# Moving the shift of three layer norms into the splits, and a group's sums to GpSimd, in a two-layer decoder step

## The chip, the cores and the metric

The kernel runs on one core of a Trainium2 chip. A core has five engines with a queue each: TensorE (PE in the profile, its weight loads PEld), VectorE (DVE), ScalarE (ACT), GpSimd (POOL) and SyncE (SP), which here issues most of the transfers. An engine works its queue strictly in order; what an instruction waits for, everything behind it waits for too. The metric is the device time of one execution in microseconds, lower is better. The median of the runs of the kernel before is 1148.62 us.

## The reference, cut to what matters

One step of a decoder of two layers on 512 prompt tokens and 8 sampled tokens, model width 1024: window attention, a convolutional FFN, gated linear attention (GLA), a second FFN. Behind each of the four stands a layer norm of a weighted residual:

```python
def layer_norm(x, g, b):
    xf = x.astype(jnp.float32)
    mu = jnp.mean(xf, -1, keepdims=True)
    var = jnp.mean(jnp.square(xf - mu), -1, keepdims=True)
    return ((xf - mu) * lax.rsqrt(var + LN_EPS) * g.astype(jnp.float32) + b.astype(jnp.float32)).astype(x.dtype)
...
        xp = layer_norm(ALPHA * xp + mp, ln_mix_g[i], ln_mix_b[i])
...
        fp, cp = conv_ffn(xp, buf0, ffn_w_up[i], ffn_conv_w[i], ffn_conv_b[i], ffn_w_down[i])
...
        xp = layer_norm(ALPHA * xp + fp, ln_ffn_g[i], ln_ffn_b[i])
```

All of it is computed in float32.

## The kernel before

**Tiles.** x lies transposed, 128 partitions by 8 rows of features (KD = 8) by tokens. The tokens are two groups, a with 256 and b with 256 + 8, each with its own tiles: x_a and x_b, and the split operands, xs_a (both parts in one tile) and xh_b, xl_b. For accuracy each float32 operand is split into a high part rounded to the matmul's format and a low part, the rest. A product of a weight unit (1024 by 128) is 8 times 3 matmul passes into one of four PSUM accumulators (accp): high weights by high rows (L173), high by low rows (L174), low weights by high rows (L175). Weights come by DMA into one of two raw buffers; ScalarE makes the high part wh (L158), VectorE the low part wl (L161), six units ahead of use.

**Order.** The work has six phases: attention, its output projection, FFN, GLA, its output projection, FFN. Inside a phase group a leads group b by four or five units; the products that b has left at the end of a phase stand before a's first of the next phase. One unit of one group is a slot. A step that has to come later is a generator, which yields the number of slots to wait. From this program order a scheduler with an engine model lists each engine's queue ahead of time; `issue_after` makes it put an instruction behind another one.

**A layer norm** has two parts. As each product of the projection ends, ln_chunk adds it to the row of x on VectorE (L219, L217 behind the FFN), which frees the accumulator; ScalarE squares the row (L237); the sum of the rows, s1, is built on VectorE (L247), the sum of the squares, s2, on GpSimd for rows 1 to 3, on VectorE for the others (L249). Both lie in tiles shown as s_a and s_b. The row 0 is handled first: a mean of it is subtracted from all rows (L232). When all eight rows are in, ln_end multiplies s1 and s2 by a matrix of 1/1024 (L256, outputs tp and pv), which gives the mean and the mean square on all partitions. ScalarE copies mu and squares it (L261, L262), VectorE makes the negative variance nv (L267), ScalarE Ln and Exp (L273, L274), VectorE a refinement of r = 1/sqrt (L275 to L277); the mean is subtracted from five rows on GpSimd, from three on VectorE (L263). Then for each row:

```python
            nc.vector.tensor_tensor(u, x[:, m], r, op=ALU.mult)
            nc.scalar.activation(g.xh[:, m], parted(u), AF.Identity, scale=sc(m), bias=bi(m))
            ts = nc.gpsimd.tensor_scalar(x[:, m], u, sc(m), bi(m), op0=ALU.mult, op1=ALU.add)
            nc.vector.tensor_tensor(g.xl[:, m], parted(x[:, m]), g.xh[:, m].bitcast(F32), op=ALU.subtract)
```

sc and bi are the norm's scale and shift, one value per partition. The low row needs x as GpSimd writes it.

**The next phase.** In an FFN the units alternate: a gate unit (its product copied to aext on ScalarE, L574; convolution, one step on ScalarE L579 and two on VectorE L580, L581; Gelu on ScalarE L588, with a table load where the table held another function) and a value unit (its product multiplied by the gate on VectorE, hprod L600, which frees the accumulator; split L198, L199). GLA starts with gla_rank (L671, L672), whose output leads to the decay (L685 to L699, with a scan on VectorE) and, with q (L715) and k (L722), to the attention product (L730). The last norm has its own code (`last`).

## Time and profile before

| | |
|---|---|
| median of 3 runs (lowest, highest) | 1148.62 us (1147.16, 1149.75) |
| the profiled execution | 1146.73 us |
| its span | 1144.7 us |
| mean granted TensorE clock | 0.992 of full speed |
| VectorE busy / ScalarE busy / GpSimd busy | 794.5 / 575.6 / 326.4 us |
| layer norms: first rows of the next phase's first product | at 168.0, 528.6, about 766.4 us of the span |

The profiled execution is one run, seen by the profiler; its time lies 1.89 us under the median. A row of a timeline gives start, duration, engine, line and operation, output and inputs by their names, and in brackets the idle time just before it with what ended it; a row with x2 or more joins consecutive instructions. A row of a source line gives the least, the median and the greatest duration in ns. DVE busy over a window doesn't count its queue's waits.

### The profile page before, as it was taken

The numbers are of one execution on the slowest core, as the hardware profiler recorded it, in microseconds if no ns is written. First come the engines' busy times: TensorE is split into PE (matmuls) and PEld (weight loads), VectorE is DVE, ScalarE is ACT, GpSimd is POOL, SyncE is SP. The second block draws the span as 40 slices with busy tenths as digits, with TensorE's granted clock in tenths as the row PEclk, the third lists the DMA queues.
The fourth block names the chain that finished last, engine by engine and source line by source line (L and its number), as shares of the span: only waits on it lengthen the run. The fifth ranks groups of instructions, "written<-read, shape, count | busy, mean of one in ns | idle before, by whom it ended". The sixth has DMA issues, their size and how long they took to land.

```text
span 1144.7 us, 22953 instructions
## 1 busy us (share of the span) xinstructions
PE 1104.2 (96%) x8806; PEld 1055.2 (92%) x8806; DVE 794.5 (69%) x1663; ACT 575.6 (50%) x1253; POOL 326.4 (29%) x556
## 2 busy tenths in 40 slices
PE   8999899999999999999899999989999999999995
PEld 8997798999999999998899999888999999999994
DVE  7897589655665566668867777799655665566657
ACT  5677457534553245435545556456524553245433
POOL 4575568100110011357300101287100110011344
PEclk9999999999999999999899999999999999999998
DMA  7553031323323233243124355341333232232222
GB/s 241 149 183 90 13 111 56 111 93 123 99 93 111 92 99 105 74 133 110 38 89 147 117 177 162 133 145 62 105 96 127 93 106 98 92 111 93 74 63 75
DMA packets 53789, 122.82 MB, mean 107 GB/s; under 512 B 6792, under 2 KB 27312, under 8 KB 53680
## 3 DMA queue, kind: packets, MB, share of 16 engines
q1 hardware_dynamic: 51664, 119.61, 32.4%
q10 hardware_dynamic: 2016, 1.75, 0.5%
q8 instruction: 69, 1.13, 0.4%
q14 instruction: 40, 0.33, 0.1%
HBM read 108.67 MB, written 8.47 MB: 102 GB/s over the span
## 4 chain that ended last, share of the span: by engine, by line
PE 70%; DVE 12%; DMA 6%; ACT 4%; POOL 4%; issue 4%; SPq 0%; ACTq 0%; DVEq 0%; POOLq 0%
PE accp L191 15%; PE accp L174 14%; PE accp L173 14%; PE accp L175 14%; PE accp L192 8%; DMA vb<-dv 3%; DVE wl L161 2%; POOL x_b L298 1%; DVE sgla L845 1%; DMA qs<-hl 1%; ACT wh L158 1%; POOL x_a L298 1%; DVE u L296 1%; PE pv L494 1%; DVE msq L276 1%
## 5 line engine op out<-in xcount | busy, mean ns | idle before, releaser
L161 DVE TENSOR_TENSOR wl<-raw,wh 128x1024 fp32r<-128x1024 f32 (+2 forms) x189 | 231.4, 1226 | 106.7 <-ACT wh L158 105.2
L158 ACT ACTIVATE wh<-raw 128x1024 fp32r<-128x1024 f32 (+2 forms) x185 | 191.9, 1037 | 215.0 <-PE accp L174 196.8
L173 PE MATMUL accp<-xh_b,wh 128*128 128x264 f32 x976 | 271.7, 279 | 2.5 <-DVE hprod L600 2.5
L174 PE MATMUL accp<-xl_b,wh 128*128 128x264 f32 x976 | 271.3, 278 | 0.2
L175 PE MATMUL accp<-xh_b,wl 128*128 128x264 f32 x976 | 270.8, 278 | 0.0
L191 PE MATMUL accp<-xs_a,wh 128*128 128x512 f32 x576 | 196.3, 382 | 0.0
L173 PEld LDWEIGHTS accp<-xh_b,wh 128*128 128x128 f32 x976 | 185.0, 190 | 3.5 <-DVE hprod L600 2.9
L174 PEld LDWEIGHTS accp<-xl_b,wh 128*128 128x128 f32 x976 | 184.9, 189 | 3.1 <-DVE xl_b L301 0.6
L175 PEld LDWEIGHTS accp<-xh_b,wl 128*128 128x128 f32 x976 | 184.8, 189 | 0.8 <-issue 0.6
L192 PE MATMUL accp<-xs_a,wl 128*128 128x256 f32 x576 | 145.4, 273 | 0.0
L173 PE MATMUL accp<-hh_b,wh 128*128 128x264 f32 x480 | 133.7, 279 | 3.3 <-ACT hh_b L198 3.3
L174 PE MATMUL accp<-hl_b,wh 128*128 128x264 f32 x480 | 134.3, 280 | 0.0
L175 PE MATMUL accp<-hh_b,wl 128*128 128x264 f32 x480 | 133.3, 278 | 0.0
L191 PEld LDWEIGHTS accp<-xs_a,wh 128*128 128x128 f32 x576 | 109.1, 189 | 11.4
L173 PE MATMUL accp<-xs_a,wh 128*128 128x256 f32 x400 | 112.3, 287 | 5.6 <-DVE x_b L219 2.1
L174 PE MATMUL accp<-xs_a,wh 128*128 128x256 f32 x400 | 112.4, 283 | 3.2 <-DVE xs_a L301 2.9
L192 PEld LDWEIGHTS accp<-xs_a,wl 128*128 128x128 f32 x576 | 110.2, 191 | 1.9
L175 PE MATMUL accp<-xs_a,wl 128*128 128x256 f32 x400 | 111.0, 280 | 0.7 <-DVE wl L161 0.5
L173 PEld LDWEIGHTS accp<-hh_b,wh 128*128 128x128 f32 x480 | 91.3, 190 | 3.8 <-ACT hh_b L198 3.6
L174 PEld LDWEIGHTS accp<-hl_b,wh 128*128 128x128 f32 x480 | 91.3, 190 | 1.4 <-issue 0.3
L175 PEld LDWEIGHTS accp<-hh_b,wl 128*128 128x128 f32 x480 | 91.3, 190 | 0.2
L202 POOL COPY hist<-aext 128x2 f32<-128x2 f32 x44 | 8.9, 203 | 284.4 <-DVE aext L578 281.3
(320 smaller groups left out, 2495.3 us busy)
## 6 DMA issues: line engine op xcount, KB each, us to landing
raw<-in_w_up SPq DMA_DIRECT2D x88, 512.0 KB, 3.4
raw<-in_w_down SPq DMA_DIRECT2D x32, 512.0 KB, 3.4
raw<-in_w_gla SPq DMA_DIRECT2D x24, 512.0 KB, 3.4
raw<-in_w_mix_o SPq DMA_DIRECT2D x16, 512.0 KB, 4.1
raw<-in_w_down SPq DMA_DIRECT2D x16, 384.0 KB, 3.1
qs<-hl SPq DMA_DIRECT2D x64, 64.0 KB, 2.1
sgla<-in_state_gla SPq DMA_DIRECT2D x16, 256.0 KB, 2.8
vb<-dv SPq DMA_DIRECT2D x16, 256.0 KB, 3.7
```

The lines of the kernel that those rows point to most:

```text
L158: nc.scalar.activation(h[:, c], r[:, c], AF.Copy)
L161: nc.vector.tensor_tensor(l[:, c], r[:, c], h[:, c].bitcast(F32), op=ALU.subtract)
L173: nc.tensor.matmul(o, h[:, ks], xh, start=k == 0, stop=False)
L174: nc.tensor.matmul(o, h[:, ks], xl, start=False, stop=False)
L175: nc.tensor.matmul(o, l[:, ks], xh, start=False, stop=k == nt - 1)
L191: both = lambda: nc.tensor.matmul(o, h[:, ks], in_turn(rs[:, k].rearrange("p t q j -> p t (q j)")), start=k == 0, stop=last)
L192: low = lambda: nc.tensor.matmul(o[:, :P], l[:, ks], in_turn(rh[:, k]), start=False, stop=False)
L276: nc.vector.scalar_tensor_tensor(q, q, 0.5, nv, op0=ALU.mult, op1=ALU.mult)
L296: nc.vector.tensor_tensor(u, x[:, m], r, op=ALU.mult)
L298: ts = nc.gpsimd.tensor_scalar(x[:, m], u, sc(m), bi(m), op0=ALU.mult, op1=ALU.add)
L494: mm = nc.tensor.matmul(pv[64 * v:64 * v + 64, b * P:(b + 1) * P], self.vtok[:, kb, 64 * v:64 * v + 64], parts[v][w][:, b], start=i == 0, ...
L845: late(nc.vector.scalar_tensor_tensor(s[:, j], vb[:, j], kraw[:, b:b + 1], s[:, j], op0=ALU.mult, op1=ALU.add))
```

## The change

For the first three norms (all but the last):

- The scaled row v = (x − mu)·sc·r is written into x itself. The high row is v + shift rounded; the low row is (v + shift) − high, made by one VectorE instruction from v. So neither needs GpSimd. The final addition x += shift stays on GpSimd, and its program place is 14 slots later (LATEB).
- Group b's sums s1 and s2 for rows 1 to 6 are on GpSimd; for row 7 on VectorE. Its two mean products come in the slot of the last row, not one later. Group a's are as before.
- For 5 units before the ends of three phases, the weights' low part comes one slot later in program order, and, as b's sums do, behind the last scaled row of group a where that row is at most 3 slots old (HOLD, `behind`).
- In group a's first FFN unit all passes with low rows come last in its product; in gla_rank for both groups too.
- The gelus of an FFN's first three gates are put behind Exp of the last norm in ScalarE's queue.
- The subtractions of the mean on GpSimd lose the hint that put them behind the group's last final pass.

```diff
@@ -52,6 +52,10 @@
+LATEB = 14
+
+HOLD = 3
@@ load_unit
-    def load_unit(self, u, pieces=1, extra=False):
+    def load_unit(self, u, pieces=1, extra=False, late=False):
...
-            nc.vector.tensor_tensor(l[:, c], r[:, c], h[:, c].bitcast(F32), op=ALU.subtract)
+            if not late:
+                nc.vector.tensor_tensor(l[:, c], r[:, c], h[:, c].bitcast(F32), op=ALU.subtract)
         self.w[u] = (h, l)
+        if late:
+            self.spawn(self.low_part(l[:, c], r[:, c], h[:, c]), 1)
+
+    def low_part(self, l, r, h):
+        with self.behind():
+            self.nc.vector.tensor_tensor(l, r, h.bitcast(F32), op=ALU.subtract)
+        yield from ()
@@ product
+        tail = g.i == 0 and u in self.phases[2::3]
...
             nc.tensor.matmul(o, h[:, ks], xh, start=k == 0, stop=False)
-            nc.tensor.matmul(o, h[:, ks], xl, start=False, stop=False)
-            nc.tensor.matmul(o, l[:, ks], xh, start=False, stop=k == nt - 1)
+            if not tail:
+                nc.tensor.matmul(o, h[:, ks], xl, start=False, stop=False)
+            nc.tensor.matmul(o, l[:, ks], xh, start=False, stop=not tail and k == nt - 1)
+        for k in range(nt) if tail else ():
+            nc.tensor.matmul(o, h[:, k * P:(k + 1) * P], in_turn(rl[:, k]), start=False, stop=k == nt - 1)
@@ ln_chunk
+    def behind(self):
+
+        return self.tc.issue_after(self.norm[0]) if self.norm and self.slot < self.norm[1] else ExitStack()
...
-        nc.vector.tensor_tensor(g.s1, x[:, 0] if m == 1 else g.s1, x[:, m], op=ALU.add)
-        eng = nc.gpsimd if m < S2P else nc.vector
-        eng.tensor_tensor(g.s2, g.s2, q, op=ALU.add)
+
+        p1, p2 = (KD - 1, KD - 1) if g.i and not last else (0, S2P)
+        with self.behind():
+            (nc.gpsimd if m < p1 else nc.vector).tensor_tensor(g.s1, x[:, 0] if m == 1 else g.s1, x[:, m], op=ALU.add)
+            (nc.gpsimd if m < p2 else nc.vector).tensor_tensor(g.s2, g.s2, q, op=ALU.add)
@@ ln_end
-        yield 1
+        yield 0 if g.i and not last else 1
...
-        with self.tc.issue_after(self.pool_mark) if self.pool_mark else ExitStack():
-            for m in range(2, KD) if last else range(NSUB):
-                sub(nc.gpsimd, m)
+        for m in range(2, KD) if last else range(NSUB):
+            sub(nc.gpsimd, m)
...
-        nc.scalar.activation(r, r, AF.Exp, scale=-0.5)
+        self.exp = nc.scalar.activation(r, r, AF.Exp, scale=-0.5).ins
...
-            u = t("u", 2)
-            nc.vector.tensor_tensor(u, x[:, m], r, op=ALU.mult)
-            nc.scalar.activation(g.xh[:, m], parted(u), AF.Identity, scale=sc(m), bias=bi(m))
-            ts = nc.gpsimd.tensor_scalar(x[:, m], u, sc(m), bi(m), op0=ALU.mult, op1=ALU.add)
-            if m == KD - 1:
-                self.pool_mark = ts.ins
-            nc.vector.tensor_tensor(g.xl[:, m], parted(x[:, m]), g.xh[:, m].bitcast(F32), op=ALU.subtract)
+            v = nc.vector.scalar_tensor_tensor(x[:, m], x[:, m], sc(m), r, op0=ALU.mult, op1=ALU.mult)
+            if m == KD - 1 and g.i == 0:
+                self.norm = v.ins, self.slot + HOLD
+            nc.scalar.activation(g.xh[:, m], parted(x[:, m]), AF.Identity, bias=bi(m))
+            nc.vector.scalar_tensor_tensor(g.xl[:, m], parted(x[:, m]), bi(m), g.xh[:, m].bitcast(F32), op0=ALU.add, op1=ALU.subtract)
+        yield LATEB
+        for m in range(KD):
+            nc.gpsimd.tensor_scalar(x[:, m], x[:, m], 1.0, bi(m), op0=ALU.mult, op1=ALU.add)
@@ ffn_gate
-        nc.scalar.activation(c[:, :n], c[:, :n], AF.Gelu)
+
+        with self.tc.issue_after(self.exp) if j < 3 else ExitStack():
+            nc.scalar.activation(c[:, :n], c[:, :n], AF.Gelu)
@@ gla_rank
-        for k in range(KD):
-            nc.tensor.matmul(o, w[:, k], in_turn(g.xh[:, k]), start=k == 0, stop=False)
-            nc.tensor.matmul(o, w[:, k], in_turn(g.xl[:, k]), start=False, stop=k == KD - 1)
+        for x in (g.xh, g.xl):
+            for k in range(KD):
+                nc.tensor.matmul(o, w[:, k], in_turn(x[:, k]), start=x is g.xh and k == 0, stop=x is g.xl and k == KD - 1)
@@ next_unit
-            self.load_unit(u, extra=extra)
+            done = u - WSLOTS
+            late = not extra and self.units[u][1] and any(e - 5 <= done < e for e in (*self.phases[2:3], *self.phases[3:4], *self.phases[5:6]))
+            self.load_unit(u, extra=extra, late=late)
```

In the queues, GpSimd behind the first norm, before (x_b and s_b are b's rows and sums; L249 adds squares, L263 subtracts the mean, L298 writes the final rows, L202 copies FFN history):

```order
L232 TENSOR_TENSOR x_b<-x_b,sa 128x264 x7
L249 TENSOR_TENSOR s_b<-s_b,sq 128x264 x3
L263 TENSOR_TENSOR x_a<-x_a,mu 128x256 x5
L298 TENSOR_SCALAR x_a<-u,par 128x256 x8
L263 TENSOR_TENSOR x_b<-x_b,mu 128x264 x5
L202 COPY hist<-aext 128x2
```

And now, at the same place, from b's fourth square sum on (L271 adds rows, L272 squares, L325 adds the shift, L286 subtracts the mean, L219 and L595 serve the FFN's history):

```order
L272 TENSOR_TENSOR s_b<-s_b,sq 128x264
L271 TENSOR_TENSOR s_b<-s_b,x_b 128x264
L325 TENSOR_SCALAR x_a<-x_a,par 128x256
L272 TENSOR_TENSOR s_b<-s_b,sq 128x264
L325 TENSOR_SCALAR x_a<-x_a,par 128x256 x6
L271 TENSOR_TENSOR s_b<-s_b,x_b 128x264
L325 TENSOR_SCALAR x_a<-x_a,par 128x256
L272 TENSOR_TENSOR s_b<-s_b,sq 128x264
L219 COPY hist<-aext 128x2
L595 MEMSET aext 128x2
L219 COPY hist<-aext 128x2
L286 TENSOR_TENSOR x_b<-x_b,mu 128x264 x5
```

What moved: the final passes of a, in one block between subtractions before, now lie among b's sums, six of them between its fifth and sixth row; b's mean is subtracted behind them as before.

VectorE ahead of b's nv behind the first norm, before (s_b sums, L301 low rows of a, L296 scaled rows of a, L161 weight splits, L267 nv):

```order
L247 TENSOR_TENSOR s_b<-s_b,x_b 128x264
L249 TENSOR_TENSOR s_b<-s_b,sq 128x264
L301 TENSOR_TENSOR xs_a<-x_a,xs_a 128x2x128
L296 TENSOR_TENSOR u<-x_a,r 128x256
L301 TENSOR_TENSOR xs_a<-x_a,xs_a 128x2x128
L296 TENSOR_TENSOR u<-x_a,r 128x256
L161 TENSOR_TENSOR wl<-raw,wh 128x1024
L267 SCALAR_TENSOR_TENSOR nv<-msq,pv 128x264
L263 TENSOR_TENSOR x_b<-x_b,mu 128x264
L301 TENSOR_TENSOR xs_a<-x_a,xs_a 128x2x128 x2
L275 TENSOR_TENSOR msq<-r 128x264
```

And now (L173 and L166 weight splits, L271 and L272 the seventh row's sums, L604 and L605 convolution steps, L289 nv):

```order
L173 TENSOR_TENSOR wl<-raw,wh 128x1024 x2
L271 TENSOR_TENSOR s_b<-s_b,x_b 128x264
L272 TENSOR_TENSOR s_b<-s_b,sq 128x264
L604 SCALAR_TENSOR_TENSOR conv<-aext,par,conv 128x256
L605 SCALAR_TENSOR_TENSOR conv<-aext,par,conv 128x256
L173 TENSOR_TENSOR wl<-raw,wh 128x1024
L604 SCALAR_TENSOR_TENSOR conv<-aext,par,conv 128x256
L166 TENSOR_TENSOR wl<-raw,wh 128x1024
L605 SCALAR_TENSOR_TENSOR conv<-aext,par,conv 128x256
L289 SCALAR_TENSOR_TENSOR nv<-msq,pv 128x264
L286 TENSOR_TENSOR x_b<-x_b,mu 128x264
L297 TENSOR_TENSOR msq<-r 128x264
```

What moved: a's scaled and low rows are all done ahead of this place; between b's last sum and nv stand four convolution steps and two weight splits of the FFN.

TensorE at the first product behind the first norm, before (L173 high by high, L174 high by low, L175 low by high; two rows more where two units alternate):

```order
L175 MATMUL accp<-hh_b,wl 128x264
L173 MATMUL accp<-xs_a,wh 128x256 x2
L174 MATMUL accp<-xs_a,wh 128x256
L175 MATMUL accp<-xs_a,wl 128x256
L173 MATMUL accp<-xs_a,wh 128x256
L174 MATMUL accp<-xs_a,wh 128x256
L175 MATMUL accp<-xs_a,wl 128x256
L173 MATMUL accp<-xs_a,wh 128x256 x2
L174 MATMUL accp<-xs_a,wh 128x256
L175 MATMUL accp<-xs_a,wl 128x256
```

And now, from the seventh feature row on (L187 high by high, L190 low by high, L192 low rows of the first unit, L189 those of other units):

```order
L187 MATMUL accp<-xs_a,wh 128x256
L190 MATMUL accp<-xs_a,wl 128x256
L187 MATMUL accp<-xs_a,wh 128x256
L190 MATMUL accp<-xs_a,wl 128x256
L187 MATMUL accp<-xs_a,wh 128x256
L192 MATMUL accp<-xs_a,wh 128x256
L189 MATMUL accp<-xs_a,wh 128x256
L190 MATMUL accp<-xs_a,wl 128x256
L187 MATMUL accp<-xs_a,wh 128x256
L192 MATMUL accp<-xs_a,wh 128x256
```

What moved: the first unit's high-row passes come as 16 in a row, and its low-row passes lie one by one between passes of the next unit.

2 lines of the change are left out of this document (1 added, 1 removed).

## The prediction

> **What bounds the kernel now.** I read the page first, then the windows around the layer norms, the list of what TensorE waited for, and the timelines of the four engines in the first of these windows.
>
> ```profile
> PE 1104.2 (96%) x8806; PEld 1055.2 (92%) x8806; DVE 794.5 (69%) x1663; ACT 575.6 (50%) x1253; POOL 326.4 (29%) x556
> ```
>
> TensorE is the bound, and the change takes no pass from it. Only time in which TensorE does nothing can be won. The windows behind the first three norms, from the first pass of the next phase on, hold much of it (columns: window, its length, then busy time and count of each engine):
>
> ```profile
> 167.90:207.00 39.10, 34.99 (x295) 33.69 (x294) 34.52 (x73) 25.90 (x48) 28.98 (x34) 1.00 0.26 82
> 528.60:556.00 27.40, 21.70 (x161) 19.47 (x160) 25.36 (x59) 16.40 (x33) 21.62 (x21) 0.95 0.18 59
> 766.40:806.40 40.00, 34.89 (x293) 33.38 (x291) 36.79 (x77) 27.61 (x51) 29.82 (x34) 1.00 0.26 86
> ```
>
> TensorE idles 39.10 − 34.99 = 4.1, 5.7 and 5.1 us there: 14.9 us, the most that this change can win. VectorE (third engine) is at 34.52 of 39.10, nearly as full, and GpSimd (last) at 28.98. The waits that lie there, all windows together (us, times, longest):
>
> ```profile
> PE accp L174 <- DVE xs_a L301: 2.9, 2, 1.5
> PE accp L173 <- DVE hprod L600: 2.5, 2, 1.3
> PE accp L173 <- DVE x_b L219: 2.1, 2, 1.1
> PE accp L672 <- DVE xl_b L301: 1.5, 2, 1.0
> PE accp L672 <- DVE xs_a L301: 1.3, 1, 1.3
> PE accp L173 <- DVE x_b L217: 1.1, 1, 1.1
> PE accp L173 <- ACT xs_a L297: 0.8, 1, 0.8
> ```
>
> Group a's low row (L301) comes late, because GpSimd must first write x (L298); b's last product waits for an accumulator that x_b += product has not emptied; and b's first product waits for the accumulator that hprod holds. In the first window these stand at:
>
> ```profile
> 168.00 0.38 PE L173 MATMUL accp<-xs_a,wh 128*128 128x256 f32 x2
> 169.74 0.38 PE L174 MATMUL accp<-xs_a,wh 128*128 128x256 f32 x1 [1.36 <-DVE xs_a L301]
> 176.64 0.28 PE L173 MATMUL accp<-xs_a,wh 128*128 128x256 f32 x1
> 176.75 0.61 PE L256 MATMUL tp<-s_b,ones_a 128*128 128x264 f32 x2
> 190.26 0.38 PE L173 MATMUL accp<-xh_b,wh 128*128 128x264 f32 x1 [1.26 <-DVE hprod L600]
> ```
>
> Passes start 0.11 us apart (176.64 to 176.75). The mean product for b's sums, tp, was not late: TensorE came to it at 176.75, and b's last square sum ended at 176.43 + 0.42 = 176.85.
>
> **The change part by part.** *The first group's rows.* The shift now goes into both splits, so xl needs no GpSimd. Before, on VectorE (start, duration):
>
> ```profile
> 162.86 1.75 DVE L161 TENSOR_TENSOR wl<-raw,wh 128x1024 fp32r<-128x1024 f32 x1
> 164.87 0.42 DVE L277 SCALAR_TENSOR_TENSOR r<-msq,r 128x256 f32<-128x256 f32 x1
> 165.21 0.75 DVE L263 TENSOR_TENSOR x_a<-x_a,mu 128x256 f32<-128x256 f32 x2
> 165.88 0.42 DVE L219 SCALAR_TENSOR_TENSOR x_b<-x_b,accp 128x264 f32<-128x264 f32 x1
> 166.22 0.76 DVE L296 TENSOR_TENSOR u<-x_a,r 128x256 f32<-128x256 f32 x2
> 176.43 0.42 DVE L249 TENSOR_TENSOR s_b<-s_b,sq 128x264 f32<-128x264 f32 x1
> 179.45 0.42 DVE L267 SCALAR_TENSOR_TENSOR nv<-msq,pv 128x264 f32<-128x264 f32 x1
> ```
>
> With the weight split ahead of r gone (late now), r ends near 163.6, the two subtractions (0.75) near 164.3, and eight scaled rows at 0.34 apart (a pair takes 0.76) end at 167.0. ScalarE's high rows follow, so the 16 high passes that now come first run from 168.0 without a wait. Behind the rows come two weight splits of 1.22 (below), to 169.4, x_b to 169.8, then the low rows, the first at about 170.4. TensorE asks for it after 16 passes, 168.0 + 16 × 0.11 = 169.8. So 0.7 us of the 1.36 stays, later low rows (0.34 apart) keep up with passes that lie between others, and the accumulator wait of about 1 us goes. TensorE reaches tp, 77 passes behind its first, at 168.0 + 77 × 0.11 + 0.7 = 177.2.
>
> *The second group's sums.* They move to GpSimd, in whose queue six of a's final passes (x += shift) now stand between b's fifth and sixth rows, one more ahead of the fifth's square, another ahead of the sixth's. Nothing of TensorE needs these passes, but what stands behind them feeds tp and pv. The prices:
>
> ```profile
> L298 POOL TENSOR_SCALAR x_a<-u,par x24: 917/1178/2483, 166.7 to 779.5; 128x256 f32<-128x256 f32 x24
> L298 POOL TENSOR_SCALAR x_b<-u,par x24: 651/1110/1322, 186.3 to 794.9; 128x264 f32<-128x264 f32 x24
> L249 POOL TENSOR_TENSOR s_b<-s_b,sq x12: 742/930/1473, 151.5 to 1117.9; 128x264 f32<-128x264 f32 x12
> L161 DVE TENSOR_TENSOR wl<-raw,wh x189: 414/1225/1769, 10.3 to 1107.5; 128x1024 fp32r<-128x1024 f32 x167, 128x768 fp32r<-128x768 f32 x16, 128x256 fp32r<-128x256 f32 x4, 128x512 fp32r<-128x512 f32 x2
> ```
>
> The trace shows this final pass only in its scaled form, 0.65 to 1.18 us. I take 1.03, between the least of a's rows (0.92) and the median of b's (1.11), since two weight splits lie beside the six on VectorE. From 169.8 (x_b's fifth row): sum 0.93, pass 1.03, square sum 0.93, six passes 6.2, sum 0.75, pass 0.65, square sum 0.75 (sixth row ready long before), then VectorE's own last addition 0.42: the sums are whole at S = 181.5, where before they were at 176.85. At 0.65 a pass S is 178.8, at 1.18 it is 183.5. TensorE stands at tp for about 4 us: a new wait, in place of three old ones.
>
> [...]
>
> ```profile
> 166.75 6.39 POOL L298 TENSOR_SCALAR x_a<-u,par 128x256 f32<-128x256 f32 x4 [3.22 <-DVE u L296]
> 166.89 1.22 DVE L161 TENSOR_TENSOR wl<-raw,wh 128x1024 fp32r<-128x1024 f32 x1
> ```
>
> *Behind S.* VectorE's queue now has, between b's last sum and nv, four convolution steps and two weight splits (before: nv came 2.6 us behind the sum, 176.85 to 179.45). And the gelus, with their table load, go ahead of b's scaled rows:
>
> ```profile
> 186.44 0.87 DVE L580 SCALAR_TENSOR_TENSOR conv<-aext,par,conv 128x256 f32<-128x256 f32 x2
> 179.90 0.43 ACT L273 ACTIVATE r<-nv 128x264 f32<-128x264 f32 x1 [0.63 <-DVE nv L267]
> 180.37 0.42 ACT L274 ACTIVATE r<-r 128x264 f32<-128x264 f32 x1
> 186.21 1.24 ACT L297 ACTIVATE xh_b<-u,par 128x264 fp32r<-128x264 f32 x2 [2.17 <-DVE u L296]
> 187.47 1.28 ACT L588 ACT_TABLE_LOAD   x1
> 188.76 0.42 ACT L588 ACTIVATE conv<-conv 128x256 f32<-128x256 f32 x1
> ```
>
> Four convolution steps at 0.4 apart and two splits at 1.15 make 4.0; nv to the end of Exp 1.34 (179.45 to 180.79); table and gelu 1.70; then hprod, two steps of r with the second hprod, r (1.45), two subtractions 0.75, a low part 0.35 and the first scaled row 0.42: S + 10.0, and the high row (0.6) S + 10.6 = 192.1. That is b's first pass, the 147th of the window in both kernels; before it stood at 190.26. The new order gains the hprod wait (gelu now first) and loses it again to the row: 192.1 − 190.26 = +1.8 us, less some 0.3 of small waits behind it: **+1.5 us** in the first window.
>
> The third window is built alike, without one wait that goes there besides (0.8, high row of a): **+0.7 us**. In the second no convolution lies behind S; what ends it is the attention product of a's first head:
>
> ```profile
> 528.63 0.27 PE L671 MATMUL accp<-xs_a,wh 128*128 128x256 f32 x1
> 549.76 0.38 PE L671 MATMUL accp<-xh_b,wh 128*128 128x264 f32 x1 [1.13 <-ACT v_a L739]
> 551.73 0.89 DVE L690 TENSOR_TENSOR_SCAN dcum<-reset,dmn 128x256 f32<-128x256 f32 x1
> 555.77 1.01 PE L730 MATMUL sc<-q_a,k_a 128*128 128x128 f32 x3 [0.23 <-DVE k_a L722]
> ```
>
> S lies 181.5 − 167.9 = 13.6 behind the window's start, as in the first. From there: weight split and decay step, nv, Ln and two Exp, r, the scan (0.89), first scaled row 6.5, high row 1.0, eight high rows at 0.6 with the low ones behind, q and k: 14.4. The product comes 28.0 behind the start, and before 555.77 − 528.63 = 27.1: **+0.9 us**.
>
> The rest costs nothing: the late weight splits are wanted six units on, counts of instructions per engine stay the same but for 27 sums that leave VectorE, the queue of weight loads doesn't change, and the last norm and what follows it keep their order. The final pass of x in b's rows is read again only by the next norm. If that cover were gone, it would cost what such a pass takes, about 1 us a row.
>
> Sum: 1.5 + 0.7 + 0.9 = +3.1 us on the profiled execution's 1146.73, 1149.8; on the median of 1148.62, **1151.7 us**. 0.2% of it, 2.3 us, is about what a measurement of this kernel can tell from no change.
>
> **The rivals.** *Quick GpSimd: faster.* The final passes, no longer tied to u, run at 0.65 us (the least of x_b's rows), and S is 178.8, 2.7 earlier. Each window then gains about 2.7 against the forecast: −1.2, −2.0 and −1.8, 5.0 in all, 1143.6 us. For it: beside idle VectorE 0.65 is measured. Against: a's passes never went under 0.92, and weight splits of 1.2 lie beside them. It decides at S = 180.1 or so, where the new wait costs as much as the old ones give back; under S = 177.2 TensorE would not wait at tp at all, and most of the 14.9 us could go: 1140 or less. *Stalls only move: no change.* S comes at 179.5 to 180.6; the sum is within 2.3 us of nothing, 1146.5 to 1150.8. For it: in before, too, each wait that was shorter stood ahead of another. *GpSimd at its contended rate: clearly slower.* At 1.18 a pass S is 183.5, and the windows cost +3.6, +2.8 and +3.0: 1158 us. For it: medians of 1178 and 1110 ns in before. *The sums' move doesn't relieve VectorE*, as its two-input steps slow down beside GpSimd's, as r's first step does in before while GpSimd subtracts (0.96, not 0.42):
>
> ```profile
> 181.82 0.96 DVE L275 TENSOR_TENSOR msq<-r 128x264 f32<-128x264 f32 x1
> ```
>
> This adds to the forecast rather than turning it, under 1 us a window, 1153.
>
> **How the numbers follow.** Forecast and both slower rivals: the forecast 0.28, contended 0.12, no relief 0.08. No change 0.26. Quick GpSimd 0.26, a quarter of it without any wait at tp. What of the forecast's own spread falls within 2.3 us of before goes to "same": slower 0.46, same 0.27, faster 0.27. For 8 in 10 the range takes in the quick case down to 1143.6 and the contended one almost whole: 1143.5 to 1157. The likeliest case alone: 1149.5 to 1154.
>
> **What would show it.** In the changed kernel's trace: the row of tp with a wait of about 4 us for GpSimd's sum of b in windows one and three, and GpSimd busy with x_a's final passes just ahead of it; the low row's wait down from 1.36 to under 1; no wait for hprod; b's first pass near 192. Wrong it is if tp shows no wait (S early), or if TensorE's idle time in the three windows falls under 12 us together.

## The result, and the profile after

| | before | changed |
|---|---|---|
| median | 1148.59 us (6 runs, 1147.16 to 1150.63) | 1160.13 us (6 runs, 1158.27 to 1163.10) |
| ratio | | 1.0102 (95%: 1.0082 to 1.0121) |
| the profiled execution, its span | 1146.73, 1144.7 us | 1162.86, 1161.0 us |
| mean granted TensorE clock | 0.992 | 0.978 |

Slower was forecast, by 3.1 us; it is 11.5 us. Instructions on TensorE are the same 8806, but its busy time grew by 13 us. In the changed kernel's page:

```profile
PE 1117.1 (96%) x8806; PEld 1064.9 (92%) x8806; DVE 792.1 (68%) x1636; ACT 567.2 (49%) x1253; POOL 322.0 (28%) x583
```

More busy time for the same passes means slower passes. To see where, I numbered TensorE's matmuls in both traces and took the same numbers ahead of and behind each window (1250 and 1600, 4100 and 4400, 5990 and 6400). Before they start at 157.44 and 203.23, 526.15 and 572.79, 763.77 and 819.66; in the changed kernel at 161.26 and 211.44, 534.35 and 583.68, 774.95 and 836.01. So the three windows lose 4.39, 2.70 and 5.16 us, 12.25 together. Another 3.82 was lost ahead of the first window, and 0.3 elsewhere. Ahead of the first window TensorE's 1250 matmuls come in the same order in both kernels, and in every other build of this study; the difference there lies between −0.15 and 3.82 us. In this execution TensorE is at half clock there up to 14.5 us (before, up to 10.4 at most) and for 6.8 us from 137.4 on (before, for 3.4 us). So the profiled execution, 2.7 us above the median of its kernel, carries a loss that the change need not have made.

What TensorE waited for in the changed kernel (us, times, longest):

```profile
PE accp L187 <- ACT xh_b L321: 6.9, 2, 3.8
...
PE accp L192 <- DVE xs_a L322: 1.5, 3, 1.1
PE accp L698 <- DVE xs_a L322: 1.5, 3, 1.1
PE accp L187 <- DVE x_b L240: 1.4, 2, 1.1
...
PE pv L279 <- DVE s_b L272: 0.7, 2, 0.4
```

The wait for hprod is gone, as forecast. A wait for b's high row stands in its place, 3.15 and 3.77 us long. The wait for b's sums, forecast at 4 us, is 0.4. In the first window:

```profile
171.82 0.27 PE L187 MATMUL accp<-xs_a,wh 128*128 128x256 f32 x1
...
183.77 0.61 PE L279 MATMUL tp<-s_b,ones_a 128*128 128x264 f32 x2
...
196.03 0.59 PE L187 MATMUL accp<-xh_b,wh 128*128 128x264 f32 x1 [3.15 <-ACT xh_b L321]
```

And this is what the wait brought with it (window, length, busy time and count of TensorE, weight loads, VectorE, ScalarE, GpSimd, and then the granted clock):

```profile
194.00:196.00 2.00, 0.00 (x0) 0.00 (x0) 2.00 (x6) 1.04 (x4) 0.03 (x1) 0.85 0.00 0
196.00:198.00 2.00, 1.97 (x9) 1.97 (x10) 2.00 (x6) 2.00 (x5) 0.00 (x0) 0.50 0.00 0
198.00:200.00 2.00, 2.00 (x11) 2.00 (x11) 2.00 (x6) 1.09 (x3) 0.52 (x1) 0.50 0.00 0
200.00:202.00 2.00, 2.00 (x12) 2.00 (x11) 2.00 (x6) 0.00 (x0) 2.00 (x1) 0.50 0.00 0
202.00:204.00 2.00, 2.00 (x18) 2.00 (x18) 1.40 (x4) 1.13 (x3) 2.00 (x4) 0.94 0.02 4
```

From 195.4 on TensorE is granted half its clock, for 6.8 us, and issues 9 to 12 passes in 2 us where it issues 18 at a clock of 0.94. That is the loss that the forecast had not priced. What came ahead of such a fall in these traces is in the last section.

Why b's row came late is in the queues of the other engines. GpSimd, then VectorE, then ScalarE, then what SyncE's weight loads waited for from 165 to 190 us:

```profile
176.56 5.79 POOL L325 TENSOR_SCALAR x_a<-x_a,par 128x256 f32<-128x256 f32 x6
182.31 0.74 POOL L271 TENSOR_TENSOR s_b<-s_b,x_b 128x264 f32<-128x264 f32 x1
```

```profile
173.99 4.71 DVE L322 SCALAR_TENSOR_TENSOR xs_a<-x_a,par,xs_a 128x256 fp32r<-128x256 f32 x7
...
184.53 0.43 DVE L272 TENSOR_TENSOR s_b<-s_b,sq 128x264 f32<-128x264 f32 x1 [1.01 <-POOL s_b L272]
184.88 0.48 DVE L604 SCALAR_TENSOR_TENSOR conv<-aext,par,conv 128x256 f32<-128x256 f32 x1
185.39 0.49 DVE L605 SCALAR_TENSOR_TENSOR conv<-aext,par,conv 128x256 f32<-128x256 f32 x1
185.80 1.22 DVE L173 TENSOR_TENSOR wl<-raw,wh 128x1024 fp32r<-128x1024 f32 x1
186.93 0.48 DVE L604 SCALAR_TENSOR_TENSOR conv<-aext,par,conv 128x256 f32<-128x256 f32 x1
187.41 1.23 DVE L166 TENSOR_TENSOR wl<-raw,wh 128x1024 fp32r<-128x1024 f32 x1
188.55 0.97 DVE L605 SCALAR_TENSOR_TENSOR conv<-aext,par,conv 128x256 f32<-128x256 f32 x1
189.45 0.41 DVE L289 SCALAR_TENSOR_TENSOR nv<-msq,pv 128x264 f32<-128x264 f32 x1
```

```profile
184.40 1.06 ACT L162 ACTIVATE wh<-raw 128x1024 fp32r<-128x1024 f32 x1 [2.60 <-DMA raw<-in_w_up]
...
187.27 0.36 ACT L284 COPY mu<-tp 128x264 f32<-128x264 f32 x1
187.52 0.39 ACT L285 ACTIVATE msq<-tp 128x264 f32<-128x264 f32 x1
```

```profile
SPq L160 <- DVE wl L173: 22.6, 4, 14.3
```

Six final passes stand between two of b's sums, as forecast. They took 0.96 us on average: five took 0.64 to 0.78, the last, beside two weight splits, 2.56. GpSimd and VectorE ran what is listed here in the order of their queues: b's sum behind the six passes began as the last of them ended (182.3 us). Beside GpSimd's sums and passes a low row of a takes 0.67 us. Behind b's last sum VectorE works without a pause up to nv: four convolution steps and two weight splits, as forecast.

One thing was overlooked. A late weight split holds its raw buffer (there are two), and no load was issued from 158 to 172.66 us; one waited 14.3 us for a late split. In the kernel before, the longest time from one load to the next there is 5.9 us. A later load, which had waited for a late split too, holds up ScalarE's high part by 2.60 us (184.40), and b's mean, ready at 184.4, is copied behind it and a second high part at 187.27. That is not what nv waited for, though: the squared mean was there at 187.52 + 0.39 = 187.91, 1.5 us ahead of nv, which followed VectorE's last convolution step with no idle time.

### The profile page after: what moved, and what is told of

Its sections match the earlier page's. It is cut to its first block, busy times and chain, and to the rows that moved or that the text cites. A ratio compares the mean times of both kernels' runs of the same rounds, so it can differ in the third digit from the quotient of the medians.

```text
span 1161.0 us, 22917 instructions
## 1 busy us (share of the span) xinstructions
PE 1117.1 (96%) x8806; PEld 1064.9 (92%) x8806; DVE 792.1 (68%) x1636; ACT 567.2 (49%) x1253; POOL 322.0 (28%) x583
## 3 DMA queue, kind: packets, MB, share of 16 engines
q8 instruction: 69, 1.13, 0.4%
## 4 chain that ended last, share of the span: by engine, by line
PE 78%; DVE 10%; DMA 4%; ACT 4%; issue 2%; POOL 1%; SPq 0%; ACTq 0%; DVEq 0%; POOLq 0%
PE accp L187 16%; PE accp L189 16%; PE accp L190 16%; PE accp L208 15%; PE accp L209 8%; DMA vb<-dv 2%; DMA qs<-hl 1%; DVE x_a L318 1%; ACT wh L162 1%; DVE xs_a L322 1%; DMA raw<-in_w_up 1%; PE pv L518 1%; DVE wl L173 1%; DVE wl L166 1%; PE sc L793 1%
## 5 line engine op out<-in xcount | busy, mean ns | idle before, releaser
L166 DVE TENSOR_TENSOR wl<-raw,wh 128x1024 fp32r<-128x1024 f32 (+2 forms) x174 | 210.5, 1212 | 115.4 <-ACT wh L162 114.8
L187 PE MATMUL accp<-xh_b,wh 128*128 128x264 f32 x976 | 272.6, 279 | 6.9 <-ACT xh_b L321 6.9
L189 PE MATMUL accp<-xl_b,wh 128*128 128x264 f32 x976 | 271.4, 278 | 0.0
L190 PE MATMUL accp<-xh_b,wl 128*128 128x264 f32 x976 | 270.8, 278 | 0.0
L187 PEld LDWEIGHTS accp<-xh_b,wh 128*128 128x128 f32 x976 | 185.8, 190 | 7.8 <-ACT xh_b L321 7.3
L189 PEld LDWEIGHTS accp<-xl_b,wh 128*128 128x128 f32 x976 | 185.2, 190 | 2.5 <-issue 0.4
L190 PEld LDWEIGHTS accp<-xh_b,wl 128*128 128x128 f32 x976 | 184.9, 189 | 0.9 <-issue 0.6
L209 PE MATMUL accp<-xs_a,wl 128*128 128x256 f32 x576 | 145.4, 273 | 0.0
L187 PE MATMUL accp<-hh_b,wh 128*128 128x264 f32 x480 | 134.1, 279 | 3.4 <-ACT hh_b L215 3.4
L189 PE MATMUL accp<-hl_b,wh 128*128 128x264 f32 x480 | 134.4, 280 | 0.0
L190 PE MATMUL accp<-hh_b,wl 128*128 128x264 f32 x480 | 133.5, 278 | 0.0
L187 PE MATMUL accp<-xs_a,wh 128*128 128x256 f32 x400 | 116.7, 295 | 4.9 <-DVE x_b L240 1.4
L190 PE MATMUL accp<-xs_a,wl 128*128 128x256 f32 x400 | 114.6, 289 | 0.5 <-DVE wl L166 0.5
L189 PE MATMUL accp<-xs_a,wh 128*128 128x256 f32 x384 | 111.5, 291 | 0.3 <-DVE xs_a L216 0.2
L187 PEld LDWEIGHTS accp<-hh_b,wh 128*128 128x128 f32 x480 | 91.6, 191 | 3.8 <-ACT hh_b L215 3.7
L189 PEld LDWEIGHTS accp<-hl_b,wh 128*128 128x128 f32 x480 | 91.5, 191 | 1.4 <-issue 0.3
L190 PEld LDWEIGHTS accp<-hh_b,wl 128*128 128x128 f32 x480 | 91.4, 190 | 0.2
L219 POOL COPY hist<-aext 128x2 f32<-128x2 f32 x44 | 10.0, 228 | 281.1 <-DVE aext L602 279.1
```

The source lines that it names most:

```text
L166: nc.vector.tensor_tensor(l[:, c], r[:, c], h[:, c].bitcast(F32), op=ALU.subtract)
L187: nc.tensor.matmul(o, h[:, ks], xh, start=k == 0, stop=False)
L189: nc.tensor.matmul(o, h[:, ks], xl, start=False, stop=False)
L190: nc.tensor.matmul(o, l[:, ks], xh, start=False, stop=not tail and k == nt - 1)
L209: low = lambda: nc.tensor.matmul(o[:, :P], l[:, ks], in_turn(rh[:, k]), start=False, stop=False)
```

## The experiments

Two tables of my own reading stand for all of them. First, where group b's chain is in the first window, in us behind group a's first pass, and what the window costs against before (by the same numbered matmuls, fills not counted); "sums" is the end of the last addition, the others are starts; "half" is half of the time at half clock:

```
                   sums   tp    mean   nv    row   b's first  window  half
before             8.85  8.75   9.45  11.45 17.76   22.26      0      0
changed           13.15 11.95  15.45  17.63 23.11   24.21      4.39   3.41
e1_fill           13.25 11.96  16.25  18.42 23.89   25.00      2.73   0
e2_pass_behind    11.07 11.11  14.90  16.87 22.67   23.78      3.97   3.41
e3_sums_back      12.44 14.34  15.22  16.48 22.73   23.84      2.61   1.71
e4_shift_only     12.22 15.41  17.75  19.15 25.37   26.48      5.33   5.12
e5_late_off       12.29 13.01  13.66  15.92 21.74   22.84      0.60   1.71
e7_nv_first       13.12 12.11  15.66  16.34 25.37   26.47      4.58   3.41
e11_late_gla      12.68 12.39  13.14  16.65 22.13   23.24      1.94   1.71
e12_late_gla_pass 12.11 13.06  13.71  15.38 21.15   22.38      1.03   1.71
```

Second, the cost of all three windows and of the stretch between the second and the third (GLA and what follows):

```
                  first  second  between  third
changed            4.39    2.70    0.29    5.16
e1_fill            2.73    3.78    1.48    3.25
e2_pass_behind     3.97    2.72    0.46    4.75
e3_sums_back       2.61   -0.97    6.41    4.88
e4_shift_only      5.33    2.27    0.15    5.77
e5_late_off        0.60    4.74    3.81    1.08
e6_rows_back       4.34    2.49   -0.19    3.75
e7_nv_first        4.58    2.88    1.58    5.70
e8_all_three       2.66    5.63    3.49    3.05
e9_before_fill    -0.01   -1.76    1.26    0.56
e10_fill_all       2.91    1.59   -0.17    3.36
e11_late_gla       1.94    1.87    0.03    0.89
e12_late_gla_pass  1.03    3.33   -0.12    2.35
```

"Between" holds no layer norm. It moves by up to 6 us as the scheduler lists GLA's queues anew: in the three builds that lose most there (e3, e5, e8) TensorE's order differs from the changed kernel's at 650 to 670 of 1590 places, in the others at 32 or fewer, and its waits there come to 5.7 or 5.8 us, not 1.9. So a total mixes the edit with that, and the windows are read one by one. Each is read from one execution, and a wait of 3.15 us came with 6.8 us at half clock in one, a longer wait with 3.4 in another (last section).

**e1_fill: the wait filled.**

```diff
+        if g.i and u in self.phases[2::3]:
+            fill = self.mtile("sc")[:, :g.n]
+            with self.tc.issue_after(self.lastmm):
+                for _ in range(FILL):
+                    nc.tensor.matmul(fill, self.ones_a, g.mu, start=True, stop=True)
...
```

> The changed kernel with six float32 products of ones by the mean of group b (into a free PSUM tile, result unused) put on TensorE just ahead of group b's first FFN pass behind the first and third norm, where TensorE waits 3.3 us. No other work is changed. Theory clock: the granted clock falls to 0.50 because of that wait and the 5 us behind it run at half speed; with the wait filled the clock stays at 1.00, b's first pass stands where it stood, and each of the two windows is 2 to 2.9 us shorter, 1155 us in all. Rival rows: the slow stretch is only TensorE waiting for the high and low rows of b, whatever the clock; then the fill changes nothing, 1160 us.

Measured: 1157.57 us, ratio to before 1.0077 (1.0055 to 1.0099), 2.6 less than the changed kernel. The row behind the fill, and the clock there:

```profile
192.84 0.38 PE L193 MATMUL accp<-xh_b,wh 128*128 128x264 f32 x1 [1.17 <-ACT xh_b L328]
```

```profile
194.00:196.00 2.00, 2.00 (x18) 1.82 (x17) 2.00 (x6) 1.78 (x5) 0.00 (x0) 1.00 0.00 0
196.00:198.00 2.00, 1.74 (x16) 1.73 (x16) 2.00 (x6) 0.38 (x1) 1.68 (x1) 1.00 0.00 0
```

The clock holds, and the first window costs exactly what b's first pass is late: 25.00 − 22.26 = 2.74, measured 2.73. In the changed kernel it is late by 1.95, and the window costs 4.39. So 2.44 of the 4.39 is the clock's. In the third window, too, the clock holds (1.00) and the cost is the lateness: b's first pass is 801.04 − 789.94 − 7.83 = 3.27 later, where 7.83 was lost ahead of the window, and the window costs 3.25. The two windows are 1.7 and 1.9 us shorter, not the 2 to 2.9 expected, as b's row itself came 0.8 later in this build. The second window and the stretch behind it lost 2.3 more, so the total fell less still: 2.6 us, with intervals that overlap.

**e2_pass_behind: a's final passes behind b's last GpSimd sum.**

```diff
+            s2i = (nc.gpsimd if m < p2 else nc.vector).tensor_tensor(g.s2, g.s2, q, op=ALU.add)
+        if g.i and m == KD - 2:
+            self.bsum = s2i.ins
...
+        with self.tc.issue_after(self.bsum):
+            for m in range(KD):
+                nc.gpsimd.tensor_scalar(x[:, m], x[:, m], 1.0, bi(m), op0=ALU.mult, op1=ALU.add)
```

> The changed kernel with group a's final passes (x += shift, GpSimd) put behind group b's last sum on GpSimd. Theory queue and port: the passes among the sums and beside the low rows cost both; without them a's seven low rows take 2.5 us rather than 4.7, the sums are whole some 4 us earlier, b's first pass waits under 1.5 us, the clock does not fall, and the time is 1146 to 1151 us. Rival tail: what comes behind the sums (convolution steps, weight splits, gelu ahead of the rows) sets the wait alone; then the wait shrinks by under 1 us and the time stays over 1157 us.

Measured: 1158.27 us, 1.0079 (1.0060 to 1.0097). The sums are whole 2.1 us earlier (11.07 for 13.15), and b's first pass comes 0.4 earlier. The rival was right: what lies behind the sums sets it. The mean stayed at 14.90, behind ScalarE's high parts, and nv behind convolution steps and splits. The expectation of 1146 to 1151 us failed: it had taken the sums for the bound.

**e3_sums_back: b's sums on the engines they had before.**

```diff
-        p1, p2 = (KD - 1, KD - 1) if g.i and not last else (0, S2P)
+        p1, p2 = 0, S2P
```

> The changed kernel with group b's sums on the engines they had before (s1 on VectorE, s2 for rows 1 to 3 on GpSimd). Theory queue and port: the final passes still run beside a's low rows, and VectorE gets nine more additions ahead of nv, so b's first pass comes no earlier: 1157 to 1162 us. Rival: GpSimd's slow sums are the loss; then the time falls to 1152 us or less.

Measured: 1161.21 us, 1.0108 (1.0086 to 1.0129): as the first theory had it in total, but not in its parts. The sums were whole 0.7 us earlier and b's first pass came 0.4 earlier. The first window cost 2.61, mostly because 3.4 us of it are at half clock where the changed kernel has 6.8. The second gained 0.97, but in another order: a's attention product came 20.89 us behind the window's start, ahead of b's first GLA pass, where before it came at 27.14. And 6.4 was lost in the stretch between. What the sums' place on GpSimd costs by itself this run doesn't show.

**e4_shift_only: the kernel before with the shift in the splits alone.**

```diff
-            u = t("u", 2)
-            nc.vector.tensor_tensor(u, x[:, m], r, op=ALU.mult)
...
+            nc.vector.scalar_tensor_tensor(x[:, m], x[:, m], sc(m), r, op0=ALU.mult, op1=ALU.mult)
+            nc.scalar.activation(g.xh[:, m], parted(x[:, m]), AF.Identity, bias=bi(m))
+            nc.vector.scalar_tensor_tensor(g.xl[:, m], parted(x[:, m]), bi(m), g.xh[:, m].bitcast(F32), op0=ALU.add, op1=ALU.subtract)
+            ts = nc.gpsimd.tensor_scalar(x[:, m], x[:, m], 1.0, bi(m), op0=ALU.mult, op1=ALU.add)
```

> The kernel before with the shift in the splits alone (scaled row in place, low row made without GpSimd, final pass on GpSimd behind it); sums, weight splits, order of passes and gelus as before. Forecast's step: the low rows' waits go in part and nothing else moves, 1145 to 1148 us. Rival port: the low rows slow down beside the final passes as in the changed kernel (0.67 us each), the waits stay, 1148 to 1151 us.

Measured: 1160.87 us, 1.0100 (1.0075 to 1.0124). Neither expectation came near. Its VectorE, TensorE and ScalarE in the first window:

```profile
166.45 2.85 DVE L295 SCALAR_TENSOR_TENSOR x_a<-x_a,par,r 128x256 f32<-128x256 f32 x7
...
171.44 0.47 DVE L297 SCALAR_TENSOR_TENSOR xs_a<-x_a,par,xs_a 128x256 fp32r<-128x256 f32 x1
```

```profile
171.97 0.58 PE L174 MATMUL accp<-xs_a,wh 128*128 128x256 f32 x1 [3.37 <-DVE xs_a L297]
```

```profile
187.91 1.28 ACT L273 ACT_TABLE_LOAD   x1
189.20 0.42 ACT L273 ACTIVATE r<-nv 128x264 f32<-128x264 f32 x1
189.64 1.28 ACT L274 ACT_TABLE_LOAD   x1
```

With GpSimd out of the low row's way, the scheduler lists all of a's scaled rows ahead of the first low row (171.44; before 169.26), and TensorE, which wants that low row for its third pass, waits 3.37 us and is granted half its clock for 6.8 us, from 171.1 on. A gelu now stands ahead of Ln and Exp, which costs two more table loads (1.28 us each) on b's chain. The other parts of the change (low passes last, the gelu hint) are aimed at just these two, and the changed kernel's total is where this one's is.

**e5_late_off: no late weight splits.**

```diff
-            late = not extra and self.units[u][1] and any(e - 5 <= done < e for e in (*self.phases[2:3], *self.phases[3:4], *self.phases[5:6]))
+            late = False and not extra and self.units[u][1] and any(e - 5 <= done < e for e in (*self.phases[2:3], *self.phases[3:4], *self.phases[5:6]))
```

> The changed kernel with no late weight splits (the low part of every unit right behind its high part in program order). Theory buffers: a late split holds its raw buffer, so the next load, the high part and with it the mean's copy behind it on ScalarE come late; without it group b's mean is copied 1 us earlier, b's first pass comes earlier, 1156 to 1159 us. Rival rows: splits ahead of group a's rows cost more than that, 1161 us or over.

Measured: 1157.95 us, 1.0072 (1.0051 to 1.0093). The mean is copied 1.8 us earlier (13.66), b's first pass comes 1.4 earlier, and the FFN windows cost 0.60 and 1.08 where they cost 4.39 and 5.16: 7.9 us won, the largest share of any part. The second window (+2.0) and the stretch behind it (+3.5) give most of it back; e11 below, with late splits there alone, loses neither. The buffers do come free sooner: the longest time from one load to the next ahead of the first window's sums falls from 14.7 to 8.3 us. But the mean is not what nv waited for here either: the squared mean was there 1.6 us ahead of it. What also changed is VectorE's queue, where one weight split stands between b's last sum and nv, not two. So these runs show what the late splits cost, and not whether it is the held buffer or the split's new place on VectorE.

**e6_rows_back: passes in the old order.**

```diff
-        tail = g.i == 0 and u in self.phases[2::3]
+        tail = False
...
+        for k in range(KD):
+            nc.tensor.matmul(o, w[:, k], in_turn(g.xh[:, k]), start=k == 0, stop=False)
+            nc.tensor.matmul(o, w[:, k], in_turn(g.xl[:, k]), start=False, stop=k == KD - 1)
```

> The changed kernel with the passes in their old order (low row right behind high row, in the first FFN unit and in GLA's first product). Theory chain: the first low row waits 3 us more, but b's first pass is set by VectorE's chain behind the sums, so TensorE only waits earlier instead of later; what it costs is a second fall of the clock, 1161 to 1164 us. Rival passes: the new order made the loss, above all in GLA's first product, then under 1157 us.

Measured: 1158.88 us, 1.0071 (1.0046 to 1.0096), with runs from 1152.86 to 1160.93; the same as the changed kernel or a little less, and below the 1161 to 1164 expected. The chain theory's first half holds (b's first pass at 24.25 and 24.21); the second clock fall that it expected came (3.4 us from 172.4 on), and the first window cost no more than in the changed kernel (4.34 and 4.39). The new order of passes gains nothing here.

**e7_nv_first: convolution steps, weight splits and decay step behind b's nv** (in the four slots of the order that follow it).

```diff
+        with self.behind_nv():
+            nc.vector.scalar_tensor_tensor(c[:, :256], a[:, 1:257], w(1), c[:, :256], op0=ALU.mult, op1=ALU.add)
+            nc.vector.scalar_tensor_tensor(c[:, :256], a[:, 0:256], w(0), c[:, :256], op0=ALU.mult, op1=ALU.add)
...
+        with self.behind_nv():
+            nc.vector.tensor_scalar(mn, zp, ba, 0.0, op0=ALU.add, op1=ALU.min)
```

> The changed kernel with hints that put the first gates' convolution steps, the weight splits and GLA's first decay step of the 4 slots behind b's last row behind b's nv on VectorE. Theory chain: nv comes up to 3 us earlier, r, the rows and b's first pass 1 to 2 us, the wait stays under 3 us and the clock falls less: 1152 to 1157 us. Rival sums: nv then waits for the mean and the sums just as long, over 1158 us.

Measured: 1162.63 us, 1.0107 (1.0084 to 1.0130): a miss. nv did come 1.3 us earlier (16.34), though not the 3 expected, because the mean still came at 15.66: with the other steps out of its way, nv waits for the mean. But the steps pushed behind nv, four convolution steps and two weight splits, now stood ahead of r, and b's first pass was 2.3 us later.

**e8_all_three: e2's and e5's edits and e7's, with the weight splits behind r.**

```diff
+                with self.behind_r():
+                    nc.vector.tensor_tensor(l[:, c], r[:, c], h[:, c].bitcast(F32), op=ALU.subtract)
...
+            late = False and not extra and self.units[u][1] and any(e - 5 <= done < e for e in (*self.phases[2:3], *self.phases[3:4], *self.phases[5:6]))
...
+        with self.tc.issue_after(self.bsum):
+            for m in range(KD):
+                nc.gpsimd.tensor_scalar(x[:, m], x[:, m], 1.0, bi(m), op0=ALU.mult, op1=ALU.add)
```

> The changed kernel with three repairs at once: a's final passes behind b's last GpSimd sum, no late weight splits, convolution steps behind b's nv and weight splits of those slots behind b's r. Theory chain and clock: the first pass of b waits under 1.5 us, the clock holds, and the three windows lose less than before the change: 1143 to 1150 us. Rival: the shift in the splits costs by itself (all scaled rows ahead of the low ones), 1153 us or over.

Measured: 1162.27 us, 1.0108 (1.0087 to 1.0130): the rival's number, for a reason that neither had. nv came at 14.40 in the first window, earliest of all builds with the change; but the first scaled row came 8.3 us behind it (5.5 in the changed kernel), as on VectorE four convolution steps and a weight split now stood between the two. GpSimd's subtractions of the mean, behind eight final passes, ended 3.8 us ahead of that row.

**e9_before_fill: the kernel before with a fill in the second window alone.**

```diff
+        fill = whole[:, 264:504]
+        prev = None
...
+            if g.i and k < KD - 1:
+                with self.tc.issue_after(mm):
+                    prev = nc.tensor.matmul(fill, self.ones_a, g.mu[:, :240], start=False, stop=False).ins
```

> The kernel before with seven float32 products of ones by the mean (240 columns, into the unused half of the accumulator, result unused) between the pairs of passes of group b's first GLA product; nothing else. Theory clock: the kernel before loses the clock itself there (0.50 from 552 to 559 us), and with TensorE busier between these passes it keeps it: the second window is 2 to 3 us shorter, 1146 to 1147 us. Rival chain: VectorE's chain to the first attention product ends that window, no change, 1149 us.

Measured: 1147.35 us (11 runs), before 1149.32 (17), 0.9977 (0.9965 to 0.9989). The two kernels' clocks there, before first:

```profile
552.00:554.00 2.00, 0.77 (x4) 0.45 (x3) 2.00 (x7) 1.13 (x3) 1.62 (x3) 0.78 0.02 4
554.00:556.00 2.00, 1.63 (x4) 1.03 (x5) 1.72 (x7) 1.32 (x5) 0.43 (x1) 0.50 0.00 0
```

```profile
552.00:554.00 2.00, 2.00 (x15) 1.90 (x14) 2.00 (x6) 0.84 (x2) 1.77 (x2) 1.00 0.02 4
554.00:556.00 2.00, 1.74 (x8) 0.96 (x6) 2.00 (x11) 1.44 (x4) 0.81 (x1) 1.00 0.00 0
```

The kernel before paid for the clock, too, and seven products whose result nobody reads make it faster by 2 us. The theory holds; the window gained 1.76, a little under the 2 to 3 expected. This is the fastest kernel of the study, ahead of both.

**e10_fill_all: the first fill, and fifteen short products in the second window.** It is e1's edit and e9's, the latter with 128 columns:

```diff
+                    with self.tc.issue_after(mm):
+                        prev = nc.tensor.matmul(fill, self.ones_a, g.mu[:, :128], start=False, stop=False).ins
```

> The changed kernel with the six products of the first fill in both FFN windows and fifteen short ones (128 columns) between the passes of group b's first GLA product. Theory clock: the second window, too, loses its half-speed stretch, 1152 to 1156 us, 2 to 5 less than with the first fill alone. Rival chain: 1157 to 1159 us, as with the first fill alone.

Measured: 1154.85 us, 1.0046 (1.0032 to 1.0060), 5.3 less than the changed kernel with nothing of its own work removed. The second window falls from 3.78 to 1.59 against the first fill alone, as its spell at half clock from 559.4 on is gone; the one from 535.6 on, ahead of the short products, is not. What is left is lateness: b's first pass in the first window is 2.9 us later than before.

**e11_late_gla: late splits ahead of GLA alone.**

```diff
-            late = not extra and self.units[u][1] and any(e - 5 <= done < e for e in (*self.phases[2:3], *self.phases[3:4], *self.phases[5:6]))
+            late = not extra and self.units[u][1] and any(e - 5 <= done < e for e in self.phases[3:4])
```

> The changed kernel with the late weight splits ahead of GLA alone, none ahead of the two FFNs. Theory buffers: in the FFN windows the late splits hold raw buffers, which holds the high parts and behind them on ScalarE b's mean; without them these two windows lose about 1 us each as with no late splits at all, the second window stays as in the changed kernel (+2.7): 1152 to 1155 us. Rival: what was gained there comes back behind GLA, 1157 us or over.

Measured: 1153.58 us, 1.0038 (1.0021 to 1.0055): inside the expected range. Against no late splits at all (e5) the second window and the stretch behind it lose 1.87 and 0.03, not 4.74 and 3.81, and of what the changed kernel loses in the FFN windows 1.94 and 0.89 are left. ScalarE's copy of b's mean now follows the gate's first convolution step, with no high part between:

```profile
182.05 0.58 ACT L603 ACTIVATE conv<-accp,par 128x256 f32<-128x256 f32 x1
182.62 0.38 ACT L284 COPY mu<-tp 128x264 f32<-128x264 f32 x1
```

**e12_late_gla_pass: the same, with a's final passes behind b's subtractions.**

```diff
+        if g.i:
+            self.bsub = si.ins
...
+        with self.tc.issue_after(self.bsub):
```

> The same as the kernel with late splits ahead of GLA alone, and a's final passes behind b's subtractions on GpSimd. Theory port and queue: a's low rows take 0.36 us each, b's sums are whole 1 to 2 us earlier and the subtractions are not held up; the windows lose no more than 1 us together besides the clock's in the second: 1147 to 1152 us. Rival: the chain behind the sums is as long as before, under 1 us is gained on the kernel without this, 1152 to 1155 us.

Measured: 1154.89 us, 1.0048 (1.0033 to 1.0064); no better than e11. In the first window b's first pass is where it was before (22.38 and 22.26); the second and third windows lose what that wins. It does show what the low rows and GpSimd's work cost each other: the low rows of a in the kernel before, in the changed kernel and in this one, and the final passes of b in the changed one, half of which run with nothing or little beside them on VectorE (least, median, greatest ns):

```profile
L301 DVE TENSOR_TENSOR xs_a<-x_a,xs_a x24: 410/431/969, 169.3 to 780.6; 128x256 fp32r<-128x256 f32 x24
```

```profile
L322 DVE SCALAR_TENSOR_TENSOR xs_a<-x_a,par,xs_a x24: 475/694/965, 174.0 to 786.3; 128x256 fp32r<-128x256 f32 x24
```

```profile
L324 DVE SCALAR_TENSOR_TENSOR xs_a<-x_a,par,xs_a x24: 472/474/979, 173.5 to 782.8; 128x256 fp32r<-128x256 f32 x24
```

```profile
L325 POOL TENSOR_SCALAR x_b<-x_b,par x24: 484/488/3479, 199.5 to 813.8; 128x264 f32<-128x264 f32 x24
```

## Why the prediction was wrong

The direction was right, and so was the chain in the first window, nearly link by link: nv 4.5 us behind the sums (forecast 4.0), b's first pass where it was forecast. The step that failed is the last one of the sum: "192.1 − 190.26 = +1.8 us", lateness taken one to one for time, with the half clock behind a wait put at nothing. The three windows lose 12.25 us, 9.15 more than forecast. Of that about 4.8 is half clock in the FFN windows, 2.1 the third window's later b row, 1.8 the second window's longer chain and 0.45 the rest of the first. Point by point, in us behind a's first pass:

- **The sums.** Forecast 13.5 (181.5 − 168.0), measured 13.15. The final passes took 0.96 on average, between the 0.65 and 1.18 that bounded them (the pass of 0.65, at 547.99 in before, lay beside a scaled row on VectorE up to 548.20, not beside an idle engine), and two weight splits did lie beside the last, as the forecast had said.
- **TensorE at the mean product.** Forecast 9.2 and a wait of 4 us there; measured 11.95 and a wait of 0.4. The low rows were taken to come 0.34 apart, and came 0.67 apart beside GpSimd's sums and final passes (in e12, without the passes, their median is 0.47 us). So TensorE waited ahead of the mean product, for the low rows, and not at it. The forecast let rows and passes side by side slow GpSimd alone, because u and the low rows of before took 0.40 to 0.46 each from 169.26 to 174.82. In before the low rows ran beside final passes, too (that of 169.26 for its whole length), and there only the pass was long: it took 1.07 us, the row 0.43. In the changed kernel both were longer, 0.69 and 0.64 us (0.47 and 0.48 with nothing or little beside them); and beside b's low rows, at 0.48 each, one final pass took 3.48. Why it goes the one way or the other no run here shows.
- **b's first pass.** Forecast 24.1, measured 24.21. The chain behind the sums was sized right. "The queue of weight loads doesn't change" was wrong in its times: the longest time from one load to the next grew from 5.9 to 14.7 us. In the first window that did not reach nv.
- **What that costs.** Forecast +1.5 in the first window, measured 4.39: 1.95 of lateness and 2.44 of half clock (e1). In the third, forecast +0.7, measured 5.16: b's first pass stands at 803.94, before at 789.94; 11.19 of these 14.00 us were lost ahead of the window, so it is 2.8 late, and 2.3 follows at half clock. The wait for a's high row (0.8 before) did not go: it is 0.70, a few passes later. And the sums there were whole 14.73 behind a's first pass, not 13.5.
- **The second window.** Forecast 28.0 behind its start, measured 566.65 − 536.82 = 29.8: the chain from the sums to the attention product took 16.7, not 14.4. VectorE first waited 0.63 for the high part of a late load, and beside GpSimd's subtractions four of its next steps took 0.65 to 0.97 (about 0.42 alone). TensorE again ran at half clock, from 560.6 on:

```profile
558.00:562.00 4.00, 3.04 (x8) 1.76 (x9) 4.00 (x13) 3.52 (x8) 0.39 (x1) 0.83 0.00 0
562.00:566.00 4.00, 3.35 (x9) 1.91 (x9) 4.00 (x10) 0.72 (x2) 4.00 (x7) 0.50 0.00 0
566.00:570.00 4.00, 3.86 (x14) 3.27 (x15) 2.54 (x6) 1.87 (x4) 0.69 (x2) 0.50 0.00 0
```

The forecast could have had it. Its own second quoted window ends in a clock of 0.95 where the others have 1.00: the kernel before lost its clock there, with no wait longer than 1.13 us. That column was quoted and not read.

The rival "GpSimd at its contended rate" gave 1158 us, close to what came, but it was not what happened: the sums were whole when the forecast had them. Its number was off besides. With 1.18 in its own sum S is 182.5 to 183.0, not 183.5, and the rival 1155 to 1156. The break-even S is 180.5 by the forecast's own +3.1 us over three windows, not 180.1. "14.9 us, the most that this change can win" counted idle time alone and left out the time at half clock, of which the kernel before has 6.8 us from 553.1 on. The waits that went (hprod) or moved (low rows, accumulators) came back in part as one wait of over 3 us, with the clock falling behind it. Of the signs, no wait for hprod and b's first pass came as written; the low row's longest wait was 1.14, not under 1, and the wait at tp was missing, though not because S was early.

What stays open: why the scheduler relists GLA's queues in e3, e5 and e8, and so how much of their totals is the edit's; and why b's row comes later in the third window than in the first. That late splits hold loads is shown by SyncE's waits; that they cost most of the two FFN windows' loss, by e5 and e11. Whether they cost it through the buffer or through their place on VectorE is not shown; a third raw buffer would test that, and was not run.

## What to carry to other kernels

In this case a wait on TensorE had two prices: its own length, and the half clock that came behind some of them, where TensorE had issued 4 to 13 passes of about 30 in the 3.4 us before (the three windows of the two kernels, last section). Waits of 2.4 to 4.8 us for b's first row in the first window brought 3.4 or 6.8 us at half clock, and waits of 1.0 to 1.5 us none. So read the clock column of every window of the profile before, and add that price to each longer wait that a change brings together. When a step is moved behind others on purpose, ask which buffer it holds and who loads into it, and what it now stands in front of. And a hint that frees one engine lets the scheduler relist all the others: compare the queues at the places that feed the bound, not only where the edit is.

## What the runs showed of the hardware

- **The clock fell with TensorE busy in part.** The 3.4 us ahead of a spell at half clock were not idle throughout. Of about 30 passes that fit, 0.11 us apart, TensorE issued 12 ahead of 553.1 in the kernel before (longest wait in them 1.00 us), and 6 ahead of 195.4, 8 ahead of 560.6, 13 ahead of 782.5 and 4 ahead of 803.0 in the changed one. The count alone is no rule: the changed kernel issued 12 in the 3.4 us from 540.1 on, and 13 in those from 174.9 and from 536.7, and kept its clock.
- **The spells lay on a grid.** In each trace they begin and end on one grid of 3.41 us and last 3.4, 6.8 or 10.2 us (but for the one that the end of the execution cuts off); where the grid lies differed from execution to execution: its first line is 0.17 us behind the span's start in the kernel before, 0.84 in the changed one, 2.1 in e3. And the longer wait did not bring the longer spell: one of 3.15 us ahead of b's first row brought 6.8 us at half clock (changed kernel), one of 4.76 us 3.4 (e3).
- **Passes of no use paid.** Seven products of 240 columns in a window that already waits won 2 us of 1149 (e9: 1147.35 and 1149.32).
- **Where the spell lies decides how its price is read.** In e7 b's first pass was 4.2 us late and the window cost 4.6: TensorE had waited 2.87 us for a weight split up to 191.87, and the spell (191.1 to 197.9) lay nearly all ahead of b's first pass at 196.89, so its price is in the 4.2. In the changed kernel the spell lay nearly all behind b's first pass, and 1.95 of lateness cost 4.39.
